# Layer 1's embedding projection placed in layer 0's mixer, and the attention's other fillers on new units

## The chip, the cores and the metric

The kernel runs as one program on one core of a Trainium2 chip. The metric is device time in microseconds (us), the median over timed runs. The core's engines each have an in-order queue: TensorE (PE in the profile, with its weight loads as PEld), VectorE (DVE), ScalarE (ACT), GpSimd (POOL) and SyncE (SP, which here only issues DMAs). An instruction that waits holds up all that stand behind it on its engine.

## The reference, cut to what matters

Two decoder layers over 512 tokens of width 1024, in float32. Layer 0 mixes with retention and an S5 state space model, layer 1 with differential attention (8 heads, two softmax maps each). Each layer ends with an embedding term that depends on an input of its own, p[i], and not on h until the gate multiplies it:

```python
    h = x
    for i in range(DEPTH):
        hn = rms_norm(h, norm_mix[i])
        mix = even_mixer(hn, ...) if i % 2 == 0 else diff_attention(hn, ...)
        h = h + mix
        h = h + swiglu(rms_norm(h, norm_ffn[i]), ffn_w_gate[i], ffn_w_up[i], ffn_w_down[i])
        gate = jax.nn.sigmoid(rms_norm(h, norm_ple[i]) @ ple_w_gate[i])
        h = h + (p[i] @ ple_w_proj[i]) * gate
    return rms_norm(h, final_norm)
```

The product `p[i] @ ple_w_proj[i]` (512x256 by 256x1024) is the embedding projection. It needs only inputs, so it can be computed anywhere ahead of the end of its layer.

## The kernel before

Everything is held as 128 partitions by tokens or features. Each float32 product is made of three matmuls of rounded parts (`mm3`, lines 120 to 123): a value is split into a high part (`whi`, `xh`, cast on ScalarE, line 99) and a low part (`wlo`, `xl`, subtracted on VectorE, line 102). Weights come by `wload` in pieces of 128x1024: a DMA into one of 3 `raw` buffers, a cast, a subtraction, into one of 5 pairs `whi`/`wlo`.

`ple_proj(L)` (line 270) makes the embedding projection of layer L. It loads 3 pieces (`pT`, and two of `ple_proj`); then each of its 4 parts, one for a block of 128 tokens, runs 12 matmuls of 128x512 (2 halves of the columns, 2 steps of the sum, 3 matmuls each), so 48 in all. ScalarE copies each half out of PSUM into a `raw` buffer (line 283), and SP writes the buffer to DRAM (line 284, `pj`). The gate step at the layer's end (`ple`, line 1144) reads it back. `lazy` turns a maker into four functions, one for each token block; the weights are loaded when the first is called.

Layer 0's mixer (`mixer0`) runs four S5 groups after each other (`s5_pre`, `s5_main`), with the input projection's parts between them, then retention over four pairs of heads (`ret_split`, `ret_head`, `ret_norm`), with one part of `ple_proj(0)` after each pair, then the gated output of S5 (`glu`) and the output projection. In one S5 group the names are: `Am` transposed into `AT` (line 574), `AT` times `U` (line 592) into a bank that VectorE rotates by `E` into `T` (line 408), scans (line 608) and rotates again into `X`; `U` times `Tm` (line 596) and `X` times `W9` (line 619) are summed; Gelu makes `Yn` (line 623), which is transposed (line 627). `E` itself is a cosine and a sine on ScalarE (lines 586 to 588). Line 549 begins the next group's kernel `dI`.

Layer 1's attention (`mixer1`) is a loop over 32 units, `u`: 8 heads with 4 query blocks each. A unit does scores (lines 851 and 852), a maximum (853) and combination (861) on VectorE, exponentials on ScalarE (856), transposes (865) and the product with the values (874, 875). A head ends with its norm (`tail`) and four transposes (`tail2`, line 902). After each unit the functions that `put(a, b, fs)` has spread over units a to b are called; these fillers are the projections of queries, keys and values (`proj(c)`), the split of the first four heads' output (`o_split`), the first half of the output projection (`wo(c, 0)`) and `ple_proj(1)`. Its second half `wo(c, 1)` follows the last head.

The written order isn't the final one. A scheduler orders each engine's queue, with the units' instructions at a higher priority than the fillers', and the pools' buffers decide what may start.

Of the kernel before, what the change touches and what calls it, by code (L numbers as in the profile page):

```python
# [67 lines left out]
def trunk(ctx: ExitStack, tc, A, out, stop=None, tap=None):  # L68
# [11 lines left out]
    def banks(**tags):  # L80
        rings.clear()
        n = 0
        for tag, w in tags.items():
            rings[tag] = [n, w, 0]
            n += w
# [4 lines left out]
    def bank(tag="mm"):  # L90
        r = rings[tag]
        n = r[0] + r[2] % r[1]
        r[2] += 1
        n, w = (f"b{n // 2}", 2) if n < 6 else (f"c{n}", 1)
        return psum.tile([P, 512], F32, tag=n, name=n, bufs=w)
# [10 lines left out]
    def wload(ap, lo_eng=V, parts=1):  # L106
        if on_pool[0] > 0:
            on_pool[0] -= 1
            lo_eng = G
        raw = rpool.tile([P, 1024], F32, tag="raw", name="raw")  # L110
        hi = wpool.tile([P, 1024], F32R, tag="whi", name="whi")
        lo = wpool.tile([P, 1024], F32R, tag="wlo", name="wlo")
        w = 1024 // parts
        for i in range(parts):
            cs = slice(i * w, (i + 1) * w)
            SP.dma_start(out=raw[:, cs], in_=ap[:, cs])
            split(hi[:, cs], lo[:, cs], raw[:, cs], lo_eng=lo_eng)
        return hi, lo

    def mm3(o, sh, sl, mh, ml, start, stop):  # L120
        PE.matmul(o, lhsT=sh, rhs=mh, start=start, stop=False)  # L121
        PE.matmul(o, lhsT=sh, rhs=ml, start=False, stop=False)  # L122
        PE.matmul(o, lhsT=sl, rhs=mh, start=False, stop=stop)  # L123
# [69 lines left out]
    def gemm_parts(xh, xl, pieces, kpp, evac, k0=0, lo_engs=(V,), last=(), ring="mm"):  # L193
        w = [wload(a, lo_engs[i % len(lo_engs)]) for i, a in enumerate(pieces)]
        wk = []
        for (hi, lo), n in zip(w, kpp):
            for j in range(n):
                wk.append((hi[:, j * 512:(j + 1) * 512], lo[:, j * 512:(j + 1) * 512]))
        n = len(wk)

        order = [k for k in range(n) if k not in last] + list(last)

        def part(t, ring=ring, *cols):
            b = bank(ring)
            cs = slice(*(cols or (0, 512)))
            for i, k in enumerate(order):
                mm3(b[:, cs], xh[:, k0 + k, t * P:(t + 1) * P], xl[:, k0 + k, t * P:(t + 1) * P],
                    wk[k][0][:, cs], wk[k][1][:, cs], i == 0, i == n - 1)
            evac(t, b, *cols)

        def all_k():
            bs = [bank() for t in range(NT)]
            for i, k in enumerate(order):
                for t in range(NT):
                    mm3(bs[t], xh[:, k0 + k, t * P:(t + 1) * P], xl[:, k0 + k, t * P:(t + 1) * P],
                        wk[k][0], wk[k][1], i == 0, i == n - 1)
            for t in range(NT):
                evac(t, bs[t])
        return part, all_k
# [9 lines left out]
    def rotary(dst, b, t, scalar, pool, bufs=2, sum_eng=G):  # L229
        t1 = pool.tile([P, 512], F32, tag="rt1", name="rt1", bufs=bufs)  # L230
        t2 = pool.tile([P, 512], F32, tag="rt2", name="rt2")
        bv = b.rearrange("p (g d) -> p g d", d=64)
        cb = cosT[:, t:t + 1, :].to_broadcast([P, 8, 64])
        s0 = sinT[:, t:t + 1, 0:32].to_broadcast([P, 8, 32])
        s1 = sinT[:, t:t + 1, 32:64].to_broadcast([P, 8, 32])
        t1v = t1.rearrange("p (g d) -> p g d", d=64)
        t2v = t2.rearrange("p (g d) -> p g d", d=64)
        V.scalar_tensor_tensor(out=t1v, in0=bv, scalar=scalar, in1=cb, op0=ALU.mult, op1=ALU.mult)
        V.scalar_tensor_tensor(out=t2v[:, :, 0:32], in0=bv[:, :, 32:64], scalar=scalar, in1=s0, op0=ALU.mult, op1=ALU.mult)
        V.scalar_tensor_tensor(out=t2v[:, :, 32:64], in0=bv[:, :, 0:32], scalar=scalar, in1=s1, op0=ALU.mult, op1=ALU.mult)  # L240
        sum_eng.tensor_tensor(out=dst, in0=t1, in1=t2, op=ALU.add)

    def residual_evac(i, c, do_sq=True, after=None):
        def ev(t, b):
            hs = hold[0][:, t, c * 512:(c + 1) * 512]
            V.tensor_tensor(out=hs, in0=b, in1=hs, op=ALU.add)  # L246
            if do_sq:
                sumsq(i, t, c)
            if after is not None:
                after(t)  # L250
        return ev
# [9 lines left out]
    def lazy(mk):  # L261
        parts = []

        def go(t):
            if not parts:
                parts.append(mk())
            parts[0](t)
        return [lambda t=t: go(t) for t in range(NT)]

    def ple_proj(L):  # L270
        def mk():
            ph, pl_ = wload(A["pT"][L])
            w = [wload(A["ple_proj"][L, c]) for c in range(2)]

            def part(t):
                pj = rpool.tile([P, 1024], F32, tag="raw", name="raw")
                for c in range(2):
                    b = bank()
                    for k in range(2):
                        ks = slice(k * 512 + t * P, k * 512 + (t + 1) * P)  # L280
                        ws = slice(k * 512, (k + 1) * 512)
                        mm3(b, ph[:, ks], pl_[:, ks], w[c][0][:, ws], w[c][1][:, ws], k == 0, k == 1)
                    AC.copy(out=pj[:, c * 512:(c + 1) * 512], in_=b)
                SP.dma_start(out=pjd[L][t], in_=pj)
            return part
        return lazy(mk)


    def mixer0():
# [447 lines left out]
                V.tensor_tensor(out=perm(ml[:, 4 + ft]), in0=src, in1=perm(f(mh[:, 4 + ft])), op=ALU.subtract)  # L737

        pf = ple_proj(0)
        banks(mm=6, sx=1, tr=1)  # L740
        pv = None
        for hp in range(4):
# [26 lines left out]
    def mixer1():  # L769
# [25 lines left out]
        def proj(c):  # L795
            def ev(t, b):
                if c < 4:
                    q = rp.tile([P, 512], F32, tag="rq", name="rq", bufs=2)
                    rotary(q, b, t, 1.0, rp, 1)
                    tb = bank("tr")  # L800
                    for j in range(4):
                        PE.transpose(out=tb[:, j * P:(j + 1) * P], in_=q[:, j * P:(j + 1) * P], identity=ident)  # L802
                    AC.copy(out=qkT[:, c, :, t * P:(t + 1) * P], in_=tb.rearrange("p (j n) -> p j n", j=4))
                else:
                    AC.copy(out=vn[:, t, (c % 2) * 512:(c % 2) * 512 + 512], in_=b)
            return gemm_parts(xh, xl, [A["w_qkv"][c, i] for i in range(4)], [2] * 4, ev)[0]
# [109 lines left out]
        def wo(c, half, *ev):  # L916
            return gemm_parts(xh, xl, [A["w_o"][c, i] for i in (2 * half, 2 * half + 1)], [2] * 2,
                              residual_evac(3, c, *ev), k0=4 * half)[0]
# [3 lines left out]
        def put(a, b, fs):  # L922
            for i, fn in enumerate(fs):
                fill.setdefault(a + i * (b - a) // len(fs), []).append(fn)

        put(0, 6, lazy(lambda: proj(1)))
        put(6, 14, lazy(lambda: proj(2)) + lazy(lambda: proj(5)))
        put(14, 18, lazy(lambda: proj(3)))
        put(21, 22, [o_split])
        put(25, 32, ple_proj(1))  # L930
        put(26, 32, lazy(lambda: wo(0, 0, False)) + lazy(lambda: wo(1, 0, False)))

        for c in (0, 4):
            part = proj(c)
# [267 lines left out]
    for name, fn in (("mix0", mixer0), ("ffn0", lambda: ffn(0, 0, 1)), ("ple0", lambda: ple(0, 1, 2)),  # L1202
                     ("mix1", lambda: pre.extend(mixer1())), ("ffn1", lambda: ffn(1, 3, 4, pre)), ("ple1", lambda: ple(1, 4, 5))):
        fn()
        if stop == name:
            finish()
            break
# [108 lines left out]
```

## Time and profile before

| what | value |
|---|---|
| median of 3 runs | 1392.57 us (1392.4 to 1394.17) |
| the profiled execution's own time | 1391.14 us |
| its span in the profile | 1389.4 us |
| mean TensorE clock granted | 0.98 of full |
| busy: TensorE, VectorE, ScalarE, GpSimd | 96%, 70%, 48%, 17% |

The profile is of one execution. Its time is 1.74 us above its span, and 1.43 us below the median. TensorE is busy nearly throughout, so what matters is where it isn't, and where it runs at a lower clock.

### The profile page before, as it was taken

How to read it: one execution, taken by the hardware profiler on the slowest of the kernel's cores; microseconds unless marked ns; L12 is line 12 of the kernel's file. 1: busy time of each engine (PE TensorE's matmuls, PEld its weight loads, DVE VectorE, ACT ScalarE, POOL GpSimd, SP SyncE). 2: the span in 40 equal slices, each digit the busy share in tenths (PEclk: the TensorE clock that was granted, in tenths of full speed). 3: DMA queues.
4: the chain of work that ended last, by engine and by line, in shares of the span. 5: the costliest groups of instructions: out<-in, count | busy, mean ns of one | idle time of the engine just before them, and what ended most of it. 6: DMA issues, size and time to landing. Idle time of an engine off the chain costs nothing. (4 is left out here: it accounts for less than half of the span.)

```text
span 1389.4 us, 20449 instructions
## 1 busy us (share of the span) xinstructions
PE 1335.5 (96%) x7938; PEld 1166.0 (84%) x7938; DVE 968.3 (70%) x1674; ACT 667.8 (48%) x1171; POOL 239.3 (17%) x231
## 2 busy tenths in 40 slices
PE   8998789899999999999999999898999999999996
PEld 6777677779998998898878888787999899889885
DVE  8998557549963985574564777887898289458453
ACT  6234556435541653353544565765555155425443
POOL 0222121122000000001253464632100000000130
PEclk9999979999999999999999999999999999999998
DMA  8532123423331333222433322323323233412431
GB/s 288 163 109 71 33 70 117 173 75 122 105 114 55 122 107 122 76 92 91 156 99 100 98 76 58 89 83 112 132 85 125 79 106 95 134 61 93 121 121 61
DMA packets 47585, 145.51 MB, mean 105 GB/s; under 512 B 10304, under 2 KB 10448, under 8 KB 47488
## 3 DMA queue, kind: packets, MB, share of 16 engines
q1 hardware_dynamic: 43040, 136.37, 30.1%
q0 software_dynamic: 4304, 7.84, 2.3%
q8 instruction: 62, 1.02, 0.3%
q14 instruction: 35, 0.29, 0.1%
q10 hardware_dynamic: 144, 0.00, 0.0%
HBM read 133.21 MB, written 8.88 MB: 102 GB/s over the span
## 5 line engine op out<-in xcount | busy, mean ns | idle before, releaser
L99 ACT CAST whi<-raw 128x1024 fp32r<-128x1024 f32 x176 | 184.5, 1050 | 223.0 <-PE b L1068 96.1
L121 PE MATMUL b<-whi,xh 128*128 128x512 f32 (+1 forms) x576 | 228.8, 402 | 8.8 <-DVE h L246 3.2
L102 DVE TENSOR_TENSOR wlo<-raw,whi 128x1024 fp32r<-128x1024 f32 x151 | 188.9, 1255 | 62.1 <-ACT whi L99 62.0
L122 PE MATMUL b<-wlo,xh 128*128 128x512 f32 (+1 forms) x576 | 229.5, 400 | 1.8 <-DVE wlo L102 1.8
L123 PE MATMUL b<-whi,xl 128*128 128x512 f32 (+1 forms) x576 | 227.4, 400 | 0.0
L102 POOL TENSOR_TENSOR wlo<-raw,whi 128x1024 fp32r<-128x1024 f32 x25 | 63.6, 2555 | 719.8 <-ACT whi L99 719.6
L121 PEld LDWEIGHTS b<-whi,xh 128*128 128x128 f32 x576 | 110.3, 192 | 35.1 <-DVE h L246 4.2
L122 PE MATMUL b<-wlo,ah 128*128 128x512 f32 x352 | 139.2, 396 | 0.0
L123 PE MATMUL b<-whi,al 128*128 128x512 f32 x352 | 138.7, 395 | 0.0
L121 PE MATMUL b<-whi,ah 128*128 128x512 f32 x352 | 138.2, 395 | 0.0
L122 PEld LDWEIGHTS b<-wlo,xh 128*128 128x128 f32 x576 | 110.4, 192 | 26.3 <-DVE wlo L102 3.2
L123 PEld LDWEIGHTS b<-whi,xl 128*128 128x128 f32 x576 | 109.8, 191 | 22.5 <-issue 0.2
L1068 PE MATMUL b<-xl,whi 128*128 128x256 f32 x456 | 127.7, 283 | 0.0
L1068 PE MATMUL b<-xh,wlo 128*128 128x256 f32 x456 | 127.1, 282 | 0.0
L1068 PE MATMUL b<-xh,whi 128*128 128x256 f32 x456 | 124.2, 283 | 0.7 <-ACT u L1073 0.7
L246 DVE TENSOR_TENSOR h<-b,h 128x512 f32<-128x512 f32 x70 | 47.6, 687 | 86.2 <-PE b L123 86.0
L1068 PEld LDWEIGHTS b<-xh,whi 128*128 128x128 f32 x456 | 84.4, 189 | 2.7 <-ACT u L1073 1.5
L1068 PEld LDWEIGHTS b<-xh,wlo 128*128 128x128 f32 x456 | 86.0, 189 | 0.5
L1068 PEld LDWEIGHTS b<-xl,whi 128*128 128x128 f32 x456 | 86.0, 189 | 0.0
L123 PEld LDWEIGHTS b<-whi,al 128*128 128x128 f32 x352 | 66.0, 188 | 15.8
L122 PEld LDWEIGHTS b<-wlo,ah 128*128 128x128 f32 x352 | 66.0, 188 | 15.0
L121 PEld LDWEIGHTS b<-whi,ah 128*128 128x128 f32 x352 | 65.6, 188 | 14.9
(363 smaller groups left out, 3217.0 us busy)
## 6 DMA issues: line engine op xcount, KB each, us to landing
raw<-in_gateup_dram SPq DMA_DIRECT2D x50, 512.0 KB, 3.6
raw<-in_down_dram SPq DMA_DIRECT2D x44, 512.0 KB, 3.8
r<-in_gateup_dram SPq DMA_DIRECT2D x38, 512.0 KB, 3.7
raw<-in_w_qkv_dram SPq DMA_DIRECT2D x24, 512.0 KB, 4.2
raw<-in_w_in_dram SPq DMA_DIRECT2D x18, 512.0 KB, 4.4
raw<-in_ple_gate_dram SPq DMA_DIRECT2D x16, 512.0 KB, 4.1
pj<-raw SPq DMA_DIRECT2D x8, 512.0 KB, 2.7
raw<-in_w_out_dram SPq DMA_DIRECT2D x8, 512.0 KB, 4.0
```

The lines of the kernel that those rows point to most:

```text
L99: AC.copy(out=hi, in_=src)
L102: lo_eng.tensor_tensor(out=lo, in0=src, in1=f(hi), op=ALU.subtract)
L121: PE.matmul(o, lhsT=sh, rhs=mh, start=start, stop=False)
L122: PE.matmul(o, lhsT=sh, rhs=ml, start=False, stop=False)
L123: PE.matmul(o, lhsT=sl, rhs=mh, start=False, stop=stop)
L246: V.tensor_tensor(out=hs, in0=b, in1=hs, op=ALU.add)
L1068: PE.matmul(o, lhsT=w[wi][:, cs], rhs=x[xi][:, k], start=start and k == 0 and i == 0, stop=k == HK - 1 and i == 2, skip_group_check=True)
```

## The change

`ple_proj(1)` is called whole in `mixer0`, after the S5 groups and ahead of retention, while the S5 stage's PSUM rings still stand. It is no longer a filler of the attention. The other fillers get other units: `proj(1)` 0 to 7 (before 0 to 6), `proj(2)` and `proj(5)` 7 to 15 (6 to 14), `proj(3)` 15 to 23 (14 to 18), `o_split` 22 (21), the first half of the output projection 24 to 32 (26 to 32). No instruction is added or taken out; later lines of the file stand 2, then 1 lower.

```diff
--- before.py
+++ after.py
@@ -737,6 +737,8 @@
                 V.tensor_tensor(out=perm(ml[:, 4 + ft]), in0=src, in1=perm(f(mh[:, 4 + ft])), op=ALU.subtract)
 
         pf = ple_proj(0)
+        for fn in ple_proj(1):
+            fn()
         banks(mm=6, sx=1, tr=1)
         pv = None
         for hp in range(4):
@@ -923,12 +925,11 @@
             for i, fn in enumerate(fs):
                 fill.setdefault(a + i * (b - a) // len(fs), []).append(fn)
 
-        put(0, 6, lazy(lambda: proj(1)))
-        put(6, 14, lazy(lambda: proj(2)) + lazy(lambda: proj(5)))
-        put(14, 18, lazy(lambda: proj(3)))
-        put(21, 22, [o_split])
-        put(25, 32, ple_proj(1))
-        put(26, 32, lazy(lambda: wo(0, 0, False)) + lazy(lambda: wo(1, 0, False)))
+        put(0, 7, lazy(lambda: proj(1)))
+        put(7, 15, lazy(lambda: proj(2)) + lazy(lambda: proj(5)))
+        put(15, 23, lazy(lambda: proj(3)))
+        put(22, 23, [o_split])
+        put(24, 32, lazy(lambda: wo(0, 0, False)) + lazy(lambda: wo(1, 0, False)))
 
         for c in (0, 4):
             part = proj(c)
```

On TensorE, the third of the four S5 groups (`_1131`, `_1137`, `_1155`, ...). Before, the rows stand in one piece:

```order
L574 MATMUL b_1131<-c_73,Am 128x128 x4
L121 MATMUL b_1573<-whi,xh 128x512
L122 MATMUL b_1573<-wlo,xh 128x512
L123 MATMUL b_1573<-whi,xl 128x512
L574 MATMUL b_1137<-c_73,Am 128x128 x4
L592 MATMUL c_1155<-U,AT 128x64 x8
L596 MATMUL c_1164<-Tm_503,U 64x128 x4
L596 MATMUL c_1165<-Tm_503,U 64x128 x4
L619 MATMUL c_1164<-W_920,X 64x128 x4
L619 MATMUL c_1165<-W_920,X 64x128 x4
```

With the change 17 matmuls of the embedding projection (tiles `b_1618`, `b_1636`, `b_1626`) stand between `b_1573` and the second set of transposes, and then:

```order
L574 MATMUL b_1137<-c_73,Am 128x128 x4
L592 MATMUL c_1155<-U,AT 128x64 x4
L596 MATMUL c_1164<-Tm_503,U 64x128 x4
L123 MATMUL b_1626<-whi,wlo 128x512
L121 MATMUL b_1644<-whi 128x512
L122 MATMUL b_1644<-wlo,whi 128x512
L123 MATMUL b_1644<-whi,wlo 128x512
L121 MATMUL b_1644<-whi 128x512
L122 MATMUL b_1644<-wlo,whi 128x512
L123 MATMUL b_1644<-whi,wlo 128x512
L121 MATMUL b_1654<-whi 128x512
L122 MATMUL b_1654<-wlo,whi 128x512
```

Ten matmuls have come between the two halves of line 592, and the last 21 stand between its second half and line 596 of `c_1165`, which is followed by line 619 as before.

On ScalarE, a little later, from the Gelu of the third group to the E of the fourth. Before:

```order
L623 ACTIVATE Yn<-c_1164 64x4x8x16
L623 ACTIVATE Yn<-c_1165 64x4x8x16
L586 ACTIVATE E<-E 128x512
L629 COPY Y<-b_1206 128x512
L587 ACT_TABLE_LOAD
L587 ACTIVATE E<-E,qpi 128x512
L588 ACTIVATE E<-E,c_87 128x512
L553 COPY dI<-b_1246 16x4x112
L553 COPY dI<-b_1254 16x4x112
L575 COPY AT<-b_1408 128x512
L575 COPY AT<-b_1414 128x512
L99 CAST Am<-qT 128x512
```

With the change:

```order
L629 COPY Y<-b_1206 128x512
L99 CAST whi<-raw 128x1024
L553 COPY dI<-b_1246 16x4x112
L99 CAST whi<-raw 128x1024
L575 COPY AT<-b_1408 128x512
L553 COPY dI<-b_1254 16x4x112
L575 COPY AT<-b_1414 128x512
L99 CAST Am<-qT 128x512
L586 ACTIVATE E<-E 128x512
L99 CAST AT<-kT 128x512
L587 ACT_TABLE_LOAD
L587 ACTIVATE E<-E,qpi 128x512
```

The casts of layer 0's own embedding weights have moved in here (the first stands just ahead of the Gelu's table load), and E has moved from ahead of the copies `dI` and `AT` to behind them and behind the first cast for retention.

On TensorE in the attention, between the end of the sixth head and that of the seventh. Before:

```order
L123 MATMUL b_8935<-whi,xl 128x512
L121 MATMUL b_8977<-whi,xh 128x512
L122 MATMUL b_8977<-wlo,xh 128x512
L851 MATMUL b_8875<-KK,QQ 128x256
L852 MATMUL b_8875<-KZ_6593,QQ 128x256
L123 MATMUL b_8977<-whi,xl 128x512
L121 MATMUL b_8977<-whi,xh 128x512
L122 MATMUL b_8977<-wlo,xh 128x512
L123 MATMUL b_8977<-whi,xl 128x512
L121 MATMUL b_8977<-whi,xh 128x512
L851 MATMUL b_8950<-KK,QQ 128x128
L852 MATMUL b_8950<-KZ_6593,QQ 128x128
```

With the change (lines 853, 854, 867, 876 and 877 are the 851, 852, 865, 874 and 875 of before):

```order
L123 MATMUL b_9051<-whi,xl 128x512
L876 MATMUL c_8693<-vv,wh 128x256
L853 MATMUL b_8840<-KK,QQ 128x384
L854 MATMUL b_8840<-KZ_6683,QQ 128x384
L877 MATMUL c_8693<-vv,wl 128x128
L853 MATMUL b_8893<-KK,QQ 128x256
L854 MATMUL b_8893<-KZ_6682,QQ 128x256
L853 MATMUL b_8950<-KK,QQ 128x128
L854 MATMUL b_8950<-KZ_6682,QQ 128x128
L867 MATMUL b_8791<-c_73,Pm 128x128 x4
L853 MATMUL b_8893<-KK,QQ 128x256
L854 MATMUL b_8893<-KZ_6683,QQ 128x256
```

Where a filler's matmuls (the output projection, `whi,xh`) stood between the scores, scores and transposes now follow each other.

## Rows read from the trace of the kernel before

**Rows 1.** the page: busy time of each engine, and its share of the span.
```profile
PE 1335.5 (96%) x7938; PEld 1166.0 (84%) x7938; DVE 968.3 (70%) x1674; ACT 667.8 (48%) x1171; POOL 239.3 (17%) x231
```

**Rows 2.** span, then busy PE, PEld, DVE, ACT, POOL; PE clock; DMA share, GB/s.
```profile
160.00:200.00 40.00, 29.33 (x160) 23.61 (x159) 25.26 (x62) 17.90 (x28) 7.00 (x14) 0.74 0.14 35
```

**Rows 3.** TensorE in order of time at the end of the S5 stage.
```profile
151.11 0.40 PE L122 MATMUL b<-wlo,xh 128*128 128x512 f32 x1
...
152.04 0.39 PE L123 MATMUL b<-whi,xl 128*128 128x512 f32 x1
...
154.97 2.08 PE L592 MATMUL c<-U,AT 128*128 128x64 f32 x16
...
165.94 3.60 PE L619 MATMUL c<-W,X 128*64 128x128 f32 x16 [5.08 <-DVE X L408]
...
174.79 1.20 PE L574 MATMUL b<-c,Am 128*128 128x128 f32 x8 [2.02 <-ACT dI L553]
...
179.73 1.33 PE L121 MATMUL b<-Am,Tm 64*128 64x512 f32 x4
...
185.06 0.80 PE L121 MATMUL b<-whi 128*128 128x512 f32 x1 [1.04 <-DVE xl L679]
...
192.79 1.96 PE L619 MATMUL c<-W,X 128*64 128x128 f32 x16
...
198.31 0.52 PE L627 MATMUL b<-c,Yn 64*128 64x64 f32 x5 [1.58 <-ACT Yn L623]
```

**Rows 4.** ScalarE in order of time, same stretch.
```profile
171.56 1.28 ACT L587 ACT_TABLE_LOAD   x1
...
173.48 0.71 ACT L588 ACTIVATE E<-E,c 128x512 f32<-128x512 f32 x1
...
176.51 0.62 ACT L99 CAST Am<-qT 128x512 fp32r<-128x512 f32 x1
```

**Rows 5.** VectorE in order of time, fourth S5 group: T, later X.
```profile
179.84 2.09 DVE L408 TENSOR_TENSOR T<-c,E 128x512 f32<-128x512 f32 x3 [1.98 <-PE c L592]
...
190.53 0.67 DVE L408 TENSOR_TENSOR X<-T,T 128x504 f32<-128x504 f32 x1
```

**Rows 6.** the page: weight splits on ScalarE and VectorE, all stages.
```profile
L99 ACT CAST whi<-raw 128x1024 fp32r<-128x1024 f32 x176 | 184.5, 1050 | 223.0 <-PE b L1068 96.1
...
L102 DVE TENSOR_TENSOR wlo<-raw,whi 128x1024 fp32r<-128x1024 f32 x151 | 188.9, 1255 | 62.1 <-ACT whi L99 62.0
```

**Rows 7.** DMA issues: size and median time to landing.
```profile
pj<-raw SPq DMA_DIRECT2D x8, 512.0 KB, 2.7
...
raw<-in_ple_proj_dram SPq DMA_DIRECT2D x4, 512.0 KB, 4.3
...
raw<-in_pT_dram SPq DMA_DIRECT2D x2, 512.0 KB, 3.8
```

**Rows 8.** same columns, attention stage, cut where the third to eighth heads end.
```profile
758.80:867.40 108.60, 108.60 (x573) 92.01 (x572) 82.89 (x196) 67.38 (x164) 50.70 (x41) 1.00 0.28 83
867.40:892.90 25.50, 25.50 (x143) 21.84 (x142) 20.08 (x54) 19.67 (x52) 16.52 (x12) 1.00 0.12 36
892.90:918.80 25.90, 21.83 (x102) 17.81 (x100) 22.40 (x52) 16.03 (x45) 12.34 (x11) 0.80 0.43 128
918.80:936.80 18.00, 18.00 (x99) 15.49 (x98) 15.88 (x45) 14.14 (x39) 8.16 (x6) 1.00 0.30 96
936.80:954.70 17.90, 16.06 (x94) 13.85 (x92) 14.59 (x32) 11.64 (x33) 3.96 (x2) 1.00 0.61 202
954.70:967.60 12.90, 11.53 (x52) 8.79 (x53) 7.54 (x22) 5.91 (x19) 2.90 (x4) 1.00 0.02 7
```

**Rows 9.** TensorE by shape, 884 to 937 us: layer 1's embedding projection.
```profile
L121 PE MATMUL b<-whi 128*128 128x512 f32 x16 | 6.5, 406 | 0.0
```

**Rows 10.** TensorE in order of time where the fifth head stalls.
```profile
896.04 0.39 PE L851 MATMUL b<-KK,QQ 128*128 128x256 f32 x1 [1.96 <-DVE mx L853]
...
901.91 0.79 PE L122 MATMUL b<-wlo,xh 128*128 128x512 f32 x1 [0.85 <-DVE wlo L102]
```

## The prediction

> **What bounds the kernel now.** I read the page's busy times first: TensorE is busy 96% of the span [rows 1], so a gain must come from the 54 us in which it isn't, or from time at the lower clock. A table of windows shows where these are. In layer 0's mixer, from 160 to 200 us, TensorE is busy 29.33 of 40 us at a granted clock of 0.74 [rows 2]; with the two levels of 1.2 and 2.4 GHz that is about half of the stretch at each. The rows in order of time show why: at the end of the S5 stage TensorE has only S5's chain left. It waits 5.08 us for X and 2.02 us for `dI`, and line 619 takes 3.60 us in one group and 1.96 in the next [rows 3]. The second place is the attention, cut at the ends of heads in [rows 8]. Through the first three heads (to 867.4) TensorE is busy throughout; from there on VectorE is nearly as busy, and the fifth head, 892.9 to 918.8, has TensorE at 21.83 of 25.90 us and a clock of 0.80. It waits there for a maximum from VectorE and for a weight's low part [rows 10].
>
> **Pace.** Four steps of 128x512 take 152.04 less 151.11, so 0.2325 us for one [rows 3]. The embedding projection's 48 matmuls (three groups like the one in [rows 9], 16 each) are 11.2 us. They leave the attention and arrive in the mixer. With them go 3 casts of 1.05 us and 3 subtractions of 1.25 us [rows 6], 8 copies out of PSUM, and 3 loads and 4 writes on SP's queue [rows 7].
>
> **Term 1, layer 0's mixer.** The 48 matmuls stand in the very gap, but not behind S5's work: 17 stand ahead of the second set of `Am` transposes (4.0 us), 10 between the halves of line 592 (2.3 us), 21 ahead of line 596's second half (4.9 us). Line 592 ended at 157.05 (154.97 and 2.08) and now ends at about 163.3. From there to line 619 it was 8.9 us; VectorE did two retention splits of 128x512 in between, each about half of a weight's 1.25 us [rows 6], which the new order puts before and behind this piece, so about 7.7, and line 619 starts at 171.0, 5.1 late. TensorE's own line meanwhile ends the projection at 168.2, so it waits some 2 us where it waited 5.08. If the clock is still full then, line 619 takes 1.96 us and not 3.60, and S5 is 3.5 late.
>
> Then comes ScalarE's queue. Layer 0's weight casts (3 of 1.05 us) now stand ahead of, and between, the copies that release TensorE, and E is made behind the first retention cast `Am`. E was done at 174.19 (173.48 and 0.71) [rows 4], with room, since VectorE's T waited for TensorE to 179.84 [rows 5]. Adding up ScalarE's queue from Yn on (at about 173): two Yn, Y, `dI` twice, `AT` twice (0.6 each), two casts of 1.05, `Am`, E, the second cast (0.6 each), a table load of 1.28, two of 0.7: 10.2 us with no wait, and some 1.5 us of waits for the transposes of line 574. So E comes at about 184.8, and T 5 us late. `Am` itself is 1.2 late at most (176.51 plus 0.62 has slack to 179.73, where its matmuls start). Behind T in VectorE's queue stand retention's maskings and splits, for which TensorE waited at 185.06 [rows 3]. Of T's 5 us, 1.6 is slack between X (ready at 191.20 [rows 5]) and line 619 of that group at 192.79, and up to 1.58 is time in which TensorE waited for its Yn at 198.31 [rows 3] and can now do retention's matmuls that were held up. I take the mixer as 2 us longer. Bounds: 6 us longer if all of T's delay and the stall behind it reach the end; 4 us shorter if the filled gap keeps the clock up, since retention's first 10 us (179.73 to about 190) ran at half rate, worth 5.
>
> What covers the rest at nothing: the casts and copies lie in ScalarE's idle time (17.90 busy of 40 us), the subtractions in VectorE's 14.7 us [rows 2]. The output is read only at the end of layer 1.
>
> **Term 2, the attention.** I counted the columns that each queue issues between heads' ends, at the pace above (0.09 us for a transpose). For TensorE, before: 104.8 us for the first three heads, then 24.4, 15.7, 17.2, 14.9 and 10.4; changed: 108.8, then 18.9, 10.4, 18.3, 9.2 and 8.5. The last head's end has 2.1 us more behind it.
> - First three heads: TensorE sets the pace (108.60 busy of 108.60 us [rows 8]), so 4.0 us longer.
> - Last five: before, 82.6 us of issue took 100.2 us. TensorE's issue falls to 65.3, and it no longer sets the pace there. VectorE was busy 80.5 us (five rows of [rows 8] added), and the same count of its queue falls from 84.5 to 78.9 nominal, so about 75.2 us. Its share of the time was 0.80 over the whole and 0.88 in the fullest head (15.88 of 18.00). At 0.80 the five take 93.9 us, at 0.88 85.5. I take 0.85, nearer the fuller end, because part of its waits came from fillers: a projection matmul that waited for its low part held TensorE up at 901.91 [rows 10]. That is 88.5, so 11.7 us shorter.
> - Behind the last head 2.1 us longer.
>
> In sum 5.6 us shorter, with bounds of 0.2 and 8.6. SP's queue loses four writes that stood between the output projection's loads; the raw buffers come free earlier, which is in the share above.
>
> **Sum.** 2.0 less 5.6 is 3.6 us. From the profiled execution's own 1391.14 that is 1387.5; it lies 1.43 us below the median, so on the median's footing 1389.0 us, 0.26% faster.
>
> **Rivals.**
> - *The late heads fall to the lower clock (no change).* TensorE's issue in heads five, seven and eight is now 28.1 us in some 45, so it pauses between scores and products. In head five of before, after waits of 1.96 us and less, the clock stood at 0.80 over 25.90 us [rows 8, 10]. If these three heads run at half rate, the five take 65.3 plus 28.1, so 93.4 us: 6.8 shorter, less the 6.1 added elsewhere, and the mixer's 2.0 turns it into 1.3 longer, 1393.9 us. For it speaks how small a wait was enough; against it that heads six to eight before, with pauses too, show 1.00. The Trainium skill, "TensorE: Matmul & The Clock Gate", Part 1, says that the default is half rate and that sustained activity releases it, which speaks against thinning out the fillers; by that rule the time is this rival's. The fifth head of before agrees (0.80), the eighth (11.53 busy of 12.90 at 1.00) does not have enough idle time to test it.
> - *Layer 0's own weights come late (slower).* Their loads now stand on SP behind layer 1's writes: three writes, a load, a write, two loads, each write waiting for a copy of the projection. Their casts stand on ScalarE ahead of S5's Gelu table load and of `dI` and `AT`. At the medians of 2.7, 3.8 and 4.3 us [rows 7] the first lands at about 171, just before Yn can start. If each of the three lands 2 to 2.5 us later, S5's chain gains about 7 us with TensorE idle: the mixer costs 9, the sum is 3.4 longer, 1396.0 us. It decides once the first load lands after about 175. For it: the chain has no slack left and ScalarE can't pass a waiting cast. Against it: DMA is at 0.14 of its time there [rows 2].
> - *The gap is filled and the clock stays up (faster still).* Term 1 at its bound of 4 shorter: 1383.0 us. It counts with the forecast.
>
> **How the numbers follow.** 0.2% of 1392.57 is 2.8 us, about what a measurement can tell from no change: faster is below 1389.8, slower above 1395.4. The forecast with the case of the clock that stays up has 0.46, the lower clock in the late heads and whatever else eats the gain without more 0.28, the late weights and larger stalls of S5 0.26. The forecast's own range is 1383 to 1391. The range for 8 in 10 is 1381 to 1398: downwards it takes both gains at nearly their bounds (4 plus 8.6 would be 1380), upwards a little past the late weights.
>
> **What the changed profile would show.** Right if the projection's matmuls run from about 154 to 168 at full clock, line 619 of the third group starts near 171, T of the fourth near 185, the last retention transposes come about 2 us later than before, and the last five heads take 86 to 91 us with VectorE at 0.83 or more. The clock rival shows as 0.7 or less in the windows of heads five, seven and eight. The late weights show as ScalarE idle ahead of `whi` near 171, released by a DMA. I would be wrong at the root if the first three heads didn't grow by 4 us, or if the last five stayed near 100 us with VectorE at 0.75: then its queue isn't what sets them, but the chain through a unit.

## The result, and the profile after

The changed kernel takes 1403.38 us (median of 4 runs, 1401.79 to 1405.01) against 1392.49 us: a ratio of 1.0073, 95% interval 1.0058 to 1.0089. It is 0.73% slower (10.9 us), on the other side of the forecast and outside its range.

The profiled execution has a span of 1401.5 us, 12.1 more than before. TensorE's wait for `vl` near 122 us, the first and the last retention transposes, the first score, the ends of the heads (as in [rows 8]) and the third FFN product divide it:

| stretch (us) | before | after | difference | forecast |
|---|---|---|---|---|
| start to the wait for `vl` | 122.06 | 123.81 | +1.75 | 0 |
| to the first retention transposes | 91.06 | 96.98 | +5.92 | +2 to the mixer's end |
| to the last retention transposes | 53.70 | 56.17 | +2.47 | 0 |
| to the first score | 491.95 | 492.25 | +0.30 | 0 |
| first three heads | 108.61 | 112.64 | +4.03 | +4.0 |
| last five heads | 100.20 | 90.87 | -9.33 | -11.7 |
| last head to the third product of layer 1's FFN | 46.57 | 53.17 | +6.60 | +2.1 |
| the rest | 375.25 | 375.61 | +0.36 | 0 |

The page's busy times (as [rows 1]), then the window of [rows 2], of the kernel after:

```profile
PE 1339.7 (96%) x7938; PEld 1167.5 (83%) x7938; DVE 962.4 (69%) x1674; ACT 671.0 (48%) x1171; POOL 241.6 (17%) x231
```
```profile
160.00:200.00 40.00, 31.41 (x182) 25.01 (x181) 31.48 (x65) 21.49 (x34) 6.70 (x13) 0.87 0.35 115
```

The stretch that looked empty is fuller and its clock higher (0.87 for 0.74), and it is still longer. TensorE in order of time shows why (as [rows 3]):

```profile
160.60 1.00 PE L592 MATMUL c<-U,AT 128*128 128x64 f32 x8
164.98 1.00 PE L592 MATMUL c<-U,AT 128*128 128x64 f32 x8
173.34 1.96 PE L619 MATMUL c<-W,X 128*64 128x128 f32 x16 [1.52 <-DVE X L408]
178.02 0.71 PE L627 MATMUL b<-c,Yn 64*128 64x64 f32 x8 [2.72 <-ACT Yn L623]
189.63 0.47 PE L121 MATMUL b<-Am,Tm 64*128 64x128 f32 x1 [1.97 <-DVE b L675]
192.24 0.79 PE L121 MATMUL b<-whi 128*128 128x512 f32 x1 [1.71 <-DVE xl L679]
206.01 0.58 PE L627 MATMUL b<-c,Yn 64*128 64x64 f32 x5 [2.90 <-ACT Yn L623]
```

The wait for X fell from 5.08 to 1.52 us, as meant. But line 592's second half ends at 165.98 instead of 157.05, 1.75 us of it from ahead of the change. Behind it the waits for Yn are longer (2.72 and 2.90 us, for 0.68 and 1.58), and so is that for retention's splits (1.71 for 1.04); that for its maskings (1.97) is not in the profile of before. ScalarE, then VectorE (as [rows 4, 5]):

```profile
174.54 1.04 ACT L99 CAST whi<-raw 128x1024 fp32r<-128x1024 f32 x1 [2.06 <-DMA raw<-in_pT_dram]
175.60 1.28 ACT L623 ACT_TABLE_LOAD   x1
188.55 0.71 ACT L588 ACTIVATE E<-E,c 128x512 f32<-128x512 f32 x1
```
```profile
188.68 0.69 DVE L408 TENSOR_TENSOR T<-c,E 128x512 f32<-128x512 f32 x1 [1.13 <-ACT E L587]
198.71 0.69 DVE L408 TENSOR_TENSOR X<-T,T 128x504 f32<-128x504 f32 x1
```

Layer 0's first weight was waited for until 174.54 with the table load and Yn behind it. E's two parts were done at 188.64 and 189.26, and T began at 188.68 instead of 179.84.

The attention by heads (as [rows 8]: columns as there, first three heads together, then the fourth to the eighth):

```profile
769.20:881.90 112.70, 112.70 (x590) 95.32 (x589) 83.09 (x204) 69.05 (x167) 50.20 (x42) 1.00 0.29 85
881.90:907.80 25.90, 22.38 (x118) 19.24 (x116) 20.81 (x54) 19.41 (x50) 16.80 (x11) 0.90 0.34 108
907.80:921.90 14.10, 13.91 (x70) 12.06 (x71) 10.70 (x29) 11.37 (x29) 7.69 (x8) 0.82 0.10 20
921.90:947.80 25.90, 21.62 (x107) 17.85 (x106) 21.18 (x51) 14.41 (x37) 15.69 (x11) 0.92 0.30 91
947.80:961.80 14.00, 12.86 (x70) 10.85 (x69) 10.37 (x40) 8.83 (x31) 1.03 (x1) 0.91 0.01 2
961.80:972.70 10.90, 9.78 (x47) 7.48 (x46) 6.82 (x20) 5.38 (x18) 1.40 (x2) 1.00 0.00 0
```

In the last five heads VectorE is busy 69.9 of 90.8 us, a share of 0.77, and the granted clock is below 1 in four heads, where it was in one. Behind the last head, two rows of VectorE before, then VectorE and TensorE of the kernel after:

```profile
972.30 0.67 DVE L102 TENSOR_TENSOR xl<-c,xh 128x512 fp32r<-128x512 f32 x1
972.89 0.67 DVE L246 TENSOR_TENSOR h<-b,h 128x512 f32<-128x512 f32 x1
```
```profile
975.67 3.52 DVE L164 SCALAR_TENSOR_TENSOR y<-h,rst,gain 128x512 f32<-128x512 f32 x2
979.11 0.68 DVE L102 TENSOR_TENSOR xl<-b,xh 128x512 fp32r<-128x512 f32 x1
979.71 1.27 DVE L246 TENSOR_TENSOR h<-b,h 128x512 f32<-128x512 f32 x2
980.91 0.68 DVE L102 TENSOR_TENSOR xl<-b,xh 128x512 fp32r<-128x512 f32 x1
981.51 1.27 DVE L102 TENSOR_TENSOR xl<-c,xh 128x512 fp32r<-128x512 f32 x2
```
```profile
979.24 0.66 PE L173 MATMUL c<-c,y 128*128 128x128 f32 x4 [1.33 <-DVE y L164]
...
980.44 0.38 PE L121 MATMUL b<-xh,whi 128*128 128x256 f32 x1 [0.31 <-DVE h L246]
982.24 0.79 PE L121 MATMUL c<-whi,xh 128*128 128x512 f32 x1 [1.41 <-DVE xl L102]
982.83 0.63 PE L122 MATMUL c<-wlo,xh 128*128 128x512 f32 x1
983.26 0.63 PE L123 MATMUL c<-whi,xl 128*128 128x512 f32 x1
```

The output projection's last matmuls need the `c` banks, which VectorE's splits (`xl<-c`) free. Before, the first of these splits stood ahead of the last two residual additions (`h<-b,h`); now it stands behind both. TensorE waits 1.33, 0.31 and 1.41 us, and its next steps of 128x512 are 0.43 us apart, the lower of its two clock levels, 1.2 GHz.

### The profile page after: what moved, and what is told of

Its sections match the earlier page's. It is cut to its first block, busy times and chain, and to the rows that moved or that the text cites. A ratio compares the mean times of both kernels' runs of the same rounds, so it can differ in the third digit from the quotient of the medians.

```text
span 1401.5 us, 20448 instructions
## 1 busy us (share of the span) xinstructions
PE 1339.7 (96%) x7938; PEld 1167.5 (83%) x7938; DVE 962.4 (69%) x1674; ACT 671.0 (48%) x1171; POOL 241.6 (17%) x231
## 5 line engine op out<-in xcount | busy, mean ns | idle before, releaser
L121 PE MATMUL b<-whi,xh 128*128 128x512 f32 (+1 forms) x576 | 229.3, 401 | 10.2 <-DVE h L246 4.4
```

## The experiments

They ran in four series, each beside runs of the kernel before, which had medians of 1390.9 to 1393.4 us there, and single runs from 1387.9 to 1398.6. So the ratios have intervals of 0.2 to 0.4%, and the stretches of the profiles tell more than the totals. A profile is of one execution: that of the spread to unit 31 is of its fastest (1393.83, median 1398.52), that of the staging and 31 together of its slowest (1401.57, median 1399.29). The letters A and B stand for other theories in the second series than in the first.

**First series: the two parts of the change apart, and the projection left out.** The first kernel has the old `put` lines without the projection, which `mixer0` calls as in the change:

```diff
+        for fn in ple_proj(1):
+            fn()
...
-        put(25, 32, ple_proj(1))
```

> Layer 1's projection in the mixer as in the changed kernel, the other fillers at the units of the kernel before. Theory A (the mixer's 10.4 us belong to the projection's place, the 7.0 us behind the last head to the new spread): the mixer is again 10 us longer, the eight heads 8 to 9 us shorter, nothing behind the last head; about 1394 us. Rival B (the 7.0 us come because the projection no longer stands among the late fillers, whatever the spread): mixer +10, heads -8, behind the last head +5 to +7; about 1400 us.

Measured 1392.43 us, ratio 0.9997 (0.9981 to 1.0012). The second has the new `put` lines with `put(25, 32, ple_proj(1))` kept, and `mixer0` as before:

> The new spread alone; the projection stays an attention filler at units 25 to 32, the mixer is that of the kernel before. Theory A: first three heads +4.0, late heads about 2 us shorter than before, behind the last head +5 to +7, mixer 0; about 1399 us. Rival B: the projection still fills the late units, so nothing is added behind the last head; about 1393 us.

Measured 1392.10 us, ratio 1.0000 (0.9984 to 1.0017). The third has the old `put` lines, the fourth the new ones, and neither calls `ple_proj(1)`:

> Layer 1's projection is left out altogether (the last stage reads layer 0's instead), the spread is the old one: what its 48 matmuls, casts and transfers cost in the attention. Theory A: 8 to 9 us less than the kernel before, nothing behind the last head; about 1384 us. Rival B: the heads give 8 us, behind the last head 5 to 7 of it are lost; about 1390 us.

Measured 1385.92 us, ratio 0.9949 (0.9932 to 0.9966).

> Layer 1's projection is left out altogether (the last stage reads layer 0's instead), the spread is the new one. Both theories: the mixer as before, heads -5.3 and +7.0 behind the last head as in the changed kernel, so about 1394 us; the difference to the changed kernel (1403.4) is the price of the place in the mixer, 9 to 10 us. If it is much less than that, the attention's state depends on where the mixer leaves the queues.

Measured 1387.33 us, ratio 0.9969 (0.9951 to 0.9986). Stretches of the table above, from the four profiles:

| kernel | `vl` to first transposes | first to last | three heads | five heads | behind the last head |
|---|---|---|---|---|---|
| mixer, old spread | 97.76 | 57.02 | 108.64 | 92.40 | 46.64 |
| new spread alone | 89.48 | 53.87 | 112.64 | 98.15 | 46.65 |
| left out, old spread | 89.49 | 57.16 | 108.62 | 92.88 | 46.72 |
| left out, new spread | 89.60 | 53.68 | 112.64 | 93.52 | 46.81 |

Both theories fell in part. Leaving out the projection gives 7.3 us in the last five heads with the old spread, 4.6 with the new one, for 11.2 us of matmuls. The new spread costs 4.0 us in the first three heads and gives 2 us or nothing in the last five. The place in the mixer costs 6.5 us by the medians of the first and the third kernel. To the first transposes the order of before takes 89.5 us in three of these kernels, and 91.06 in the profile of before: one order varies by some 1.6 us there. And none of the four has the 6.6 us behind the last head: they belong neither to the spread nor to the missing projection as such.

**Second series: ScalarE's late weights, the order behind the last head, another place.** In the first, layer 1's results go to two `rt1` buffers, so that `raw` is free for layer 0's weights:

```diff
-                pj = rpool.tile([P, 1024], F32, tag="raw", name="raw")
...
+                    half = own.tile([P, 512], F32, tag="rt1", name="rt1", bufs=2)
+                    AC.copy(out=half, in_=b)
+                    SP.dma_start(out=pjd[L][t][:, c * 512:(c + 1) * 512], in_=half)
```

> As the first experiment (projection in the mixer, old spread), but layer 1's results are staged in the two rt1 buffers, free at that time, so that the raw buffers are free for layer 0's weights as soon as layer 1's are cast; layer 0's casts then stand ahead of S5's last part on ScalarE. Theory A (the mixer's loss is layer 0's late weights in ScalarE's queue): E of the fourth group is done by about 176 us instead of 189.3, its T starts at 180 to 182 instead of 188.7, the first retention transposes come at 212 to 215 us instead of 220, and the total is about 1387 us. Rival B (the gap holds no 48 matmuls, whatever ScalarE does): the first retention transposes still come at 219 to 221 us; about 1392 us.

Measured 1391.28 us, ratio 0.9978 (0.9965 to 0.9990). TensorE, ScalarE and VectorE of this kernel (its line numbers are 6 higher: 625 is 619, 594 is 588, 414 is 408):

```profile
174.39 3.18 PE L625 MATMUL c<-W,X 128*64 128x128 f32 x16 [2.63 <-DVE X L414]
```
```profile
182.46 0.70 ACT L594 ACTIVATE E<-E,c 128x512 f32<-128x512 f32 x1
```
```profile
187.13 2.09 DVE L414 TENSOR_TENSOR T<-c,E 128x512 f32<-128x512 f32 x3 [0.30 <-PE c L598]
```

E is 6.1 us earlier than in the changed kernel, and T only 1.6: now it waits for TensorE's line 592 (here 598). The first transposes come 96.0 us after the wait for `vl` (97.0 in the changed kernel, 97.8 in the first experiment, which has the same spread). Theory A fell: the late weights were there, but TensorE's own chain was late by nearly as much beside them.

```diff
-        put(24, 32, lazy(lambda: wo(0, 0, False)) + lazy(lambda: wo(1, 0, False)))
+        put(24, 31, lazy(lambda: wo(0, 0, False)) + lazy(lambda: wo(1, 0, False)))
```

> The changed kernel with one number changed: the output projection's first half is spread over units 24 to 30 and not 24 to 31. In the instruction order this puts the split of the c banks on VectorE ahead of the two residual additions again, as in the kernel before. Theory A (the 6.6 us behind the last head are that order: TensorE waits for a bank and its clock falls): from the last head's transposes to the third stage's first product 46.6 to 46.8 us instead of 53.2; the mixer as in the changed kernel; about 1397 us. Rival B (they come from the weights, whose buffers come free late without the projection's five fillers): the stretch stays at 51 to 53 us; about 1403 us.

Measured 1398.52 us, ratio 1.0040 (1.0023 to 1.0056); 46.81 us behind the last head. VectorE and TensorE there:

```profile
974.59 0.67 DVE L102 TENSOR_TENSOR xl<-c,xh 128x512 fp32r<-128x512 f32 x1
975.18 0.67 DVE L246 TENSOR_TENSOR h<-b,h 128x512 f32<-128x512 f32 x1
975.78 0.67 DVE L102 TENSOR_TENSOR xl<-c,xh 128x512 fp32r<-128x512 f32 x1
```
```profile
973.72 0.66 PE L173 MATMUL c<-c,y 128*128 128x128 f32 x4 [1.26 <-DVE y L164]
...
975.37 0.45 PE L121 MATMUL c<-whi,xh 128*128 128x512 f32 x1
975.88 0.39 PE L123 MATMUL c<-whi,xl 128*128 128x512 f32 x1
```

The first split of a `c` bank stands ahead of both additions, TensorE waits once, and its clock stays up. Theory A holds.

The next has the calls of `ple_proj(1)` behind `pv()` and ahead of `glu()`:

> Layer 1's projection behind the retention, ahead of the gated unit, old spread. TensorE is idle 7 us from 250 to 300 us there. Theory A (what counts is whether the casts and loads stand in a queue that others wait for): the first retention transposes at 212 to 214 us as before, since its casts can't come ahead of S5; the last ones later by part of the 11.2 us; 4 to 8 us dearer than without the projection, 1390 to 1394 us. Rival B (any place in the mixer costs as much as the place ahead of the retention): 6.5 us dearer, but the first transposes already late.

Measured 1398.14 us, ratio 1.0029 (1.0019 to 1.0039). The first transposes come after 91.1 us, as before, but from the last ones to the first score it is 495.5 us for 492.0, and the last five heads, in an order that no other kernel has, take 98.1 us, which I can't explain. Then the staging and the spread to 31 together:

> Both mended: the staging in rt1 and the new spread with its end at 31. Theory A: both losses are gone: the mixer within 2 us of before, heads 5 us shorter, behind the last head 46.7 us; about 1388 us, 0.3% faster than before. Rival B: at least one of the losses stays; 1393 us or more.

Measured 1399.29 us, ratio 1.0036 (1.0021 to 1.0050): behind the last head 46.6 us, but 98.0 us to the first transposes and 95.5 for the last five heads. Up to the first transposes this kernel has the order of the one with the staging alone, which took 96.0: so early weights gave nothing there that stands out of what one order varies by.

**Third and fourth series: the order on TensorE.** With `on_pool[0] = 3` ahead of the calls, GpSimd makes the low parts of layer 1's projection weights. They come later, and TensorE's order then has 4 of the 48 matmuls ahead of line 592's second half, where 27 stood.

> The staging in rt1 of the experiment before, and the three low parts of layer 1's projection weights on GpSimd instead of VectorE. They come later by this, and in the instruction order TensorE then has 4 of the 48 matmuls ahead of line 592's second half instead of 27, 26 behind it and 18 behind line 596. Theory C (S5's chain is held up twice, by the projection's matmuls ahead of its steps on TensorE and by layer 0's late casts ahead of its steps on ScalarE; either alone costs the mixer 7 us): with both mended line 619 of the third group starts at 168 to 170 us instead of 173.3, the first retention transposes come at 214 to 216, the total is 1386 to 1389 us. Theory D (the order on TensorE alone counts): the same. Theory E (48 more matmuls cost the mixer 7 us wherever they stand): transposes at 219 to 221, 1391 to 1392 us.

Measured 1392.87 us, ratio 0.9993 (0.9981 to 1.0005); 96.6 us.

> The low parts on GpSimd as in the kernel before it, but the results are staged in the raw buffers as in the changed kernel, so that layer 0's weights come late again. Theory C (each of the two hold-ups alone costs about 7 us): E of the fourth group is late through ScalarE's queue, the first retention transposes at 218 to 221 us; 1391 to 1393 us. Theory D (the order on TensorE alone counts): 214 to 216 us, as in the kernel before it; 1386 to 1389 us. Theory E: 219 to 221 in both.

Measured 1389.16 us, ratio 0.9967 (0.9955 to 0.9979); 95.5 us. It beats the kernel before, and the changed one, by its median, with 108.65, 90.25 and 46.64 us in the attention. In both the first transposes stand at 219.5 to 219.6 us. Theories C and D fell, E holds: the whole projection ahead of the retention costs the mixer 4.4 to 6.9 us over the 91.06 of before in all its orders (6 to 8.5 over the 89.5 of the other kernels). VectorE's X and TensorE's line 619 of this kernel show why the better order didn't help:

```profile
168.20 0.68 DVE L408 TENSOR_TENSOR X<-T,T 128x504 f32<-128x504 f32 x1
```
```profile
172.14 1.96 PE L619 MATMUL c<-W,X 128*64 128x128 f32 x16
```

X was ready at 168.88, and line 619 began 3.3 us later, without a wait: the 44 matmuls behind line 592's second half take 10.2 us, where TensorE had waited 6.8 us before (1.73 for T and 5.08 for X). Then, in a fourth series, half of it:

```diff
+        for fn in ple_proj(1)[:2]:
+            fn()
...
+        put(27, 32, ple_proj(1)[2:])
```

> Half of layer 1's projection (24 matmuls) in the mixer ahead of the retention, the other half among the attention's late fillers (its weights loaded a second time), old spread. All 24 stand ahead of line 592's second half in TensorE's order, none in the wait for X behind it. Measured from TensorE's wait for vl at 122 us (runs differ there by up to 2 us before the change begins) to the first retention transposes: 91.0 us before, 97.0 in the changed kernel. Theory F (a matmul ahead of the chain's steps costs its own time, only one inside a wait is free): about 96 us, total 1394 to 1396. Theory G (only the sum of TensorE's work against its idle time counts: 5.6 us of work into 10 us of waits): 91 to 92 us, total 1389 to 1391.

Measured 1396.47 us, ratio 1.0032 (1.0012 to 1.0052); 95.99 us.

> The same half, with the low parts of its weights on GpSimd: now 4 of the 24 matmuls stand ahead of line 592's second half and 20 behind it, inside the wait for X. Theory F: 91 to 92.5 us from the wait for vl to the first retention transposes. Theory G: the same as the other half, 91 to 92. If it stays at 96, neither holds. Besides, behind the last head VectorE's order has by itself fallen as in the changed kernel (the two residual additions ahead of the c banks' splits): by the theory that this order makes the 6.6 us there, the stretch from the last head's transposes to the third stage's first product is 52 to 54 us and the total 1394 to 1398; if it is 46.7, the order is not the cause.

Measured 1392.62 us, ratio 1.0014 (1.0001 to 1.0027); 91.45 us. The last five heads, with the other half among their fillers, take 100.8 and 94.4 us. TensorE's line 592, second half, and its wait for X in the half ahead of the chain, then in the half inside the wait:

```profile
162.97 1.00 PE L592 MATMUL c<-U,AT 128*128 128x64 f32 x8
...
174.51 3.67 PE L619 MATMUL c<-W,X 128*64 128x128 f32 x16 [6.87 <-DVE X L408]
```
```profile
158.70 1.10 PE L592 MATMUL c<-U,AT 128*128 128x64 f32 x8
...
168.96 3.67 PE L619 MATMUL c<-W,X 128*64 128x128 f32 x16 [3.52 <-DVE X L408]
```

The same 24 matmuls cost 4.5 us more where they stand ahead of line 592. Its second half ends 41.5 us after the wait for `vl` in the one and 36.9 in the other: 4.6 us, the time of the 20 matmuls. In the first the wait for X doesn't shrink either, it grows from 5.08 to 6.87 us, because VectorE makes low parts of layer 0's weights inside X's chain:

```profile
168.78 1.23 DVE L102 TENSOR_TENSOR wlo<-raw,whi 128x1024 fp32r<-128x1024 f32 x1 [0.35 <-ACT whi L99]
...
172.64 1.22 DVE L102 TENSOR_TENSOR wlo<-raw,whi 128x1024 fp32r<-128x1024 f32 x1
```

In the second only one such part stands there. So the two kernels differ in VectorE's order too, which no run tried alone; it can account for the 1.4 us by which the way from line 592 to 619 is longer (10.5 for 9.2 us), not for the 4.6. Theory F holds for the half, G falls. The second half kernel has the bad order behind the last head again, and pays for it: 52.99 us, by the same wait, in its TensorE row

```profile
971.10 0.80 PE L121 MATMUL c<-whi,xh 128*128 128x512 f32 x1 [1.41 <-DVE xl L102]
```

## Why the prediction was wrong

- **Line 619 of the third group, at 171.0.** It came at 173.34, or 171.6 without the 1.75 us by which this execution was late before any moved instruction. In fourteen kernels, with the same order on every engine up to there, the wait for `vl` lies between 122.06 and 124.36 us, so that offset isn't the change's. This step was right, and so was the full clock (1.96 us).
- **T 5 us late, most of it absorbed: the step that failed in the mixer.** Less the offset T was 7.1 us late, not 5. The sum of ScalarE's queue was added up too low (its parts make 10.8 us, not 10.2) and left out the 2.06 us for which ScalarE waited for a weight; and TensorE's chain was late by nearly as much on its own (T still 5.7 us late, less that run's offset of 1.62, with the weights early). And of it only 1.2 us were absorbed, not 3: the term was 2.0 and measured 5.9. The slack I counted lay in waits that themselves moved with the chain. The gain of a clock that stays up came only in part: from 160 to 200 us the clock rose from 0.74 to 0.87, but behind the stall for the maskings the matmuls ran at the lower level again (0.79 us for a 128x512 at 192.24, as at 185.06 before).
- **What this was at its root.** 27 of the 48 matmuls stood ahead of a step of S5's chain. I had added their 6.3 us (line 592 ended 7.2 us late, less the offset), but then set them against waits behind that step. Their place is not all of it: with 4 ahead of the step the mixer was still 4.4 to 5.5 us longer than before, since the 44 behind it were more than the wait there holds. Only half of the projection, with 20 of its matmuls in the wait, cost the mixer nothing clear of what one order varies by (91.45 us).
- **The late weights, the slower rival.** Its sign came nearly as forecast: ScalarE idle ahead of `whi`, released by a DMA, at 174.54 against a point of 175. Its price did not: with the weights early the mixer takes 96.0 and 98.0 us, with them late 96.5 to 97.8 in three kernels of the changed order. A sign that fits doesn't show that its cause is the only one.
- **First three heads, +4.0.** Measured +4.03; the same 112.64 us in all five kernels with the new spread, 108.6 to 108.7 in all nine with the old.
- **Last five heads, 88.5 us at a VectorE share of 0.85.** Measured 90.87 at 0.77: mis-sized by 2.4 us, and the pace is not VectorE's alone. Without the projection among their fillers the five take 90.3 to 92.9 us with the old spread in five kernels, 98.1 in a sixth, and 90.9 to 95.5 with the new one in four; with it, 100.2 and 98.15. So most of the gain is the projection's leaving. What the spread gives there for its 4.0 us ahead is 2 us or none, less than the orders of the same fillers differ by. Three kernels with one order on every engine agree (92.8 to 92.9 us), so these differences come from the order.
- **The clock in the late heads, the rival of no change.** It shows at 0.82 to 0.92 in four heads, not at 0.7 or less in three: in direction right, in size not. "TensorE: Matmul & The Clock Gate", Part 1, of the Trainium skill pointed that way, and these rows agree. What part of the 2.4 us it explains was not tried. The first kernel of the first series and the second of the third differ in these heads by the order of a few VectorE instructions alone: their fifth heads take 20.1 us at a clock of 0.77 and 18.0 at 0.83, and the other four agree, so order and clock together made 2.1 us there.
- **Behind the last head, +2.1.** Measured +6.60. The 4.5 us that are over come from a place of the order at which I had not looked: VectorE's additions ahead of the `c` banks' splits. This is the second step that failed: I had counted the columns there and not read VectorE's order. Shown twice: one number in the spread takes it away, and the forecast 2.1 with it (46.81 us), and a kernel that was changed elsewhere brings it back (52.99).
- **The retention stretch, 2.47 us longer.** Not the change's. GpSimd's `rr` of the third pair took 4.21 us, for 2.48 in six of the kernels. The kernel before and the one that leaves the projection out have the same order on every engine there, and show 53.70 and 57.16 us.

Sum of what is the change's in this profile: 5.92, 0.30, 4.03, -9.33, 6.60 and 0.36, so 7.9 us; 4.2 us more lie in the two stretches that vary by themselves. The medians are 10.9 us apart; the 5.92 is measured from the slow end of what the order of before takes (89.5 to 91.1 us), and from its fast end the sum would be 9.5. Against the forecast of 3.6 us shorter, the mixer's term was short by 3.9 us, the place behind the last head by 4.5, the last five heads by 2.4.

## What to carry to other kernels

A gap on an engine is filled only by work that stands behind the last step ahead of it and in front of the waiting one; the same work some instructions earlier delays the chain by its full time, and the gap stays. And it takes no more work than the gap is long: what is over holds up the waiting step. So read in the final order, engine by engine, where the moved instructions land, and also at the places to which the change gave no new work: a scheduler reorders those too, and here that cost about as much as the mixer. Slack found in a trace is good for a delay only if its end does not hang on the chain that is delayed.

## What the runs showed of the hardware

One GpSimd instruction on 128x8 elements, `rr` of the third pair of heads, took 2.48 us or 4.08 to 4.21 us, beside VectorE's subtractions on the same stretch. GpSimd of the changed kernel, then of the kernel with the spread to 31:

```profile
265.32 4.21 POOL L126 TENSOR_TENSOR rr<-vr,mhalf 128x8 f32<-128x8 f32 x1 [23.51 <-DVE vr L705]
```
```profile
264.01 2.48 POOL L126 TENSOR_TENSOR rr<-vr,mhalf 128x8 f32<-128x8 f32 x1 [23.52 <-DVE vr L705]
```

In the six kernels at 2.48 the first to the last retention transposes take 53.7 to 53.9 us, in the seven at 4.08 to 4.21 it is 55.8 to 57.2 (the projection behind retention has another order there). A 128x1024 subtraction on GpSimd took 6.99 us at 134 us of the first experiment with low parts on GpSimd, and 2.36 each for two at 153. One of VectorE's that began beside these two took 4.82 us, where 1.25 is the mean, and ended 1.1 us after them. GpSimd, then VectorE:

```profile
133.87 6.99 POOL L102 TENSOR_TENSOR wlo<-raw,whi 128x1024 fp32r<-128x1024 f32 x1 [6.31 <-ACT whi L99]
...
153.42 4.72 POOL L102 TENSOR_TENSOR wlo<-raw,whi 128x1024 fp32r<-128x1024 f32 x2
```
```profile
154.42 4.82 DVE L102 TENSOR_TENSOR wlo<-raw,whi 128x1024 fp32r<-128x1024 f32 x1 [5.01 <-ACT whi L99]
```

The Trainium skill, "SBUF — State Buffer", "Terms" and "Who interferes with whom", says that a VectorE instruction with two SBUF inputs and a GpSimd instruction that reads SBUF contend for a shared pair of ports, by an exclusive lock that is held for a whole instruction. VectorE's 4.82 us agree with a wait until GpSimd's two were done, and the 1.7 us between the two durations of `rr` with a wait for one or two more of VectorE's instructions; no run here takes either engine's instructions away, so the cause is argued, not shown.
